# Attention scores: three 64-row products per head, the two heads in turn, in place of two 128-row products per head

## The chip, the core and the metric

The kernel runs on one core of a Trainium2 chip. TensorE multiplies: a load puts up to 128 rows by 128 columns of the first operand into the array, then the second operand streams through it, up to 512 columns, and the result goes to a bank of PSUM. VectorE, ScalarE and GpSimd do the rest of the arithmetic, and queues on SyncE, GpSimd and ScalarE issue DMAs. The metric is device time of one launch in microseconds (us), the median of several runs.

## What is computed

A trunk of two layers on 512 tokens of width 1024. Layer 0 mixes with an mLSTM (4 heads of 192) beside memory attention, layer 1 with band attention (12 heads of 64, on keys and values shared through one projection) beside memory attention. Memory attention has 4 heads of 64 and 256 memory tokens. Each mixer ends in an output projection, and a gated MLP with a short convolution follows. The part that concerns us, cut from the reference:

```python
# band attention, per chunk of queries (own chunk and 8 before)
s = jnp.einsum('bqhd,bkhd->bhqk', qc, kc).astype(jnp.float32) * scale + bias
s = jnp.where(valid, s, -jnp.inf)
p = jax.nn.softmax(s, axis=-1).astype(vc.dtype)
...
# memory attention
s = jnp.einsum('bshd,bmhd->bhsm', q, mk).astype(jnp.float32) * (MEM_HEAD_DIM ** -0.5)
p = jax.nn.softmax(s, axis=-1).astype(mv.dtype)
```

With at most 512 tokens and a band of 9 chunks of 64, every query sees all earlier keys, so band attention works here as causal attention by blocks.

## The kernel before

Activations stay transposed: a tile has 128 features on the partitions and the 512 tokens along the free axis. A float32 value is carried as two parts of a shorter format (type `fp32r`), a high part and the remainder, and a product of two float32 operands becomes three products: high by high, high by low, low by high (`mm3`, L192). Weights come in by DMA, ScalarE casts the high part and VectorE subtracts for the low one (`split`, L139, its two operations L140 and L141), and TensorE runs through hundreds of such triples (L194, L195, L196).

A head of 64 features fills only half of the 128 rows. Two heads share one tile of queries and one of keys: head 0 on partitions 0 to 63, head 1 on 64 to 127 (`HEADS`). The kernel before fills the array with the parts. `head_keys` (L587) builds for each head one tile that holds the keys' high part on the head's own half and the low part on the other. `head_queries` (L577) builds for each head two tiles: the high part of the queries on both halves, and the low part on the head's own half with zeros (a GpSimd memset, L580) on the other. `head_scores` (L594) then needs two products over 128 rows: the first gives high by high plus high by low, the second low by high. One block of scores, that is one token tile of 128 queries for both heads, is four products at L600, called by `scores` (L633): first both of head 0, then both of head 1, each head into its own bank of PSUM (pool tag `sc`, three banks).

Who calls it:

- `memory_attention` (L638), four times, with 256 keys. It works in two rounds of two token tiles (`softmax`, L646); both tiles of a head go to one bank, and the softmax on VectorE and ScalarE (L654 to L660) starts when both are there.
- `band_attention` (L1389), six times, once for each pair of heads, with token tile T reading the first (T + 1) x 128 keys: 128, 256, 384 and 512 columns. VectorE adds the bias and takes the maximum (L1406), ScalarE takes the exponential (L1410).
- The mLSTM heads call `head_scores` directly for the tile that two heads share, with keys and queries swapped. The change leaves these calls, `head_keys` and `head_queries` in place for them.

Queries come from `queries` (L625): those of layer 0 straight from PSUM, those of layer 1 first multiplied by a row of the norm. Keys come from `project_pair` (L1365, band) and `load_memory_kv` (L602, memory).

The order of work: each attention is a generator whose `yield`s mark places where filler may go. `weave(job, filler, each)` runs the job and after each yield lets `each` times the yielded number (1 for a bare `yield`) of filler steps be issued; the filler is projection products, mostly triples for other tiles. The order in which this issues the operations is not the last word: outside the stages marked `manual_schedule` the compiler's planner reorders each engine's instructions by its own reckoning of when operands and buffers are ready, so that projection products may come between the four products of a block.

Of the kernel before, what the change touches and what calls it, by code (L numbers as in the profile page):

```python
# [10 lines left out]
F32R = mybir.dt.float32r  # L11
I32 = mybir.dt.int32
AF = mybir.ActivationFunctionType
ALU = mybir.AluOpType
AX = mybir.AxisListType

P = 128
D = 1024
S = 512
# [7 lines left out]
HD = 64  # L27
# [22 lines left out]
def f(ap):  # L50
    return ap.bitcast(F32)
# [3 lines left out]
def trunk(  # L55
# [18 lines left out]
    nc = tc.nc  # L74
    V, A, G = nc.vector, nc.scalar, nc.gpsimd
# [14 lines left out]
    def sb(tag, shape, dtype=F32):  # L90
        count[0] += 1
        return pool.tile(shape, dtype, tag=tag, name=f"{tag}{count[0]}", bufs=bufs[tag])

    def ps(tag):
        count[0] += 1
        return psum.tile([P, S], F32, tag=tag, name=f"p{tag}{count[0]}", bufs=pbufs[tag])
# [6 lines left out]
    def small(n=4, dtype=F32):  # L103
        smalls[0] += 1
        i = smalls[0] % 26
        return sb("s0" if i < 6 else "s1" if i < 12 else "s2", [P, 16], dtype)[:, :n]
# [28 lines left out]
    HEADS = (slice(0, HD), slice(HD, P))  # L135
# [3 lines left out]
    def split(hi, lo, src, on_act=True, pinned=False):  # L139
        high = A.copy(hi, src) if on_act else V.tensor_copy(hi, src)  # L140
        low = V.tensor_tensor(out=lo, in0=src, in1=f(hi), op=ALU.subtract)  # L141
        if pinned:
            pin(high)
            pin(low)
# [53 lines left out]
    def project(w, c0, act, tag="mm"):  # L198


        n = len(act)
        wh, wl = weights(rows(w, c0, P), n, P)
        o = ps(tag)
        for k in range(n):
            mm3(o, wh[:, k, :], wl[:, k, :], act[k][0], act[k][1], k == 0, k == n - 1)
            yield
        return o
# [250 lines left out]
    def value_weights(hf, u):  # L458
        n = AW // 2
        ex = rows(a_w_in, 4 * AW, 2 * AH, 2 * u, 2 * u + 2) if hf else None  # L460
        return load(rows(a_w_in, 2 * AW + hf * n, n, 2 * u, 2 * u + 2), 2, n, ex)

    with tc.manual_schedule(engines={mybir.EngineType.PE, mybir.EngineType.Activation, mybir.EngineType.DVE}):
# [56 lines left out]
        for q in range(KT // 2):  # L520
            k = 2 * q
# [39 lines left out]
        raw = value_weights(1, 0)  # L561
# [15 lines left out]
    def head_queries(t, scale=1.0):  # L577
        qs, ls = ([sb("u", [P, S], F32R) for _ in range(2)] for _ in range(2))
        for h, r in enumerate(HEADS):
            G.memset(f(ls[h])[HEADS[1 - h], :], 0.0)  # L580
            A.activation(qs[h][r, :], t[r, :], AF.Copy, scale=scale)
            V.scalar_tensor_tensor(ls[h][r, :], t[r, :], scale, f(qs[h])[r, :], op0=ALU.mult, op1=ALU.subtract)
        for h, r in enumerate(HEADS):
            A.copy(qs[h][HEADS[1 - h], :], f(qs[h])[r, :])
        return qs, ls

    def head_keys(t):  # L587
        ks = [sb("u", [P, S], F32R) for _ in range(2)]
        for h, r in enumerate(HEADS):
            A.copy(ks[h][r, :], t[r, :])  # L590
            V.tensor_tensor(out=ks[h][HEADS[1 - h], :], in0=t[r, :], in1=f(ks[h])[r, :], op=ALU.subtract)
        return ks

    def head_scores(o, h, q, tsl, k, c, first, keys_first=False):  # L594

        for i, part in enumerate(q):
            a, b = part[h][:, tsl], k[h][:, c]
            if keys_first:
                a, b = b, a
            nc.tensor.matmul(o, a, b, start=first and i == 0, stop=i == 1)  # L600

    def load_memory_kv(l):  # L602
        raw = sb("wr", [P, D])
        nc.sync.dma_start(raw, spill[l])
        k = head_keys(raw[:, :S])
        vs = []
        for m in range(2):
            v = sb("u", [P, S], F32R).rearrange("p (h c) -> p h c", h=4)
            src = raw[:, S + m * MEM : S + (m + 1) * MEM].rearrange("p (h c) -> p h c", h=4)
            split(v[:, :, :HD], v[:, :, HD:], src)  # L610
            vs.append(v)
        return k, vs


    def values(outs):

        s, t = sb("t", [P, S]), sb("t", [P, S])
        for o, r in zip(outs, HEADS):
            A.copy(t[r, :], o[HD:, :])
            V.tensor_tensor(out=s[r, :], in0=o[:HD, :], in1=t[r, :], op=ALU.add)  # L620
        hi, lo = sb("u", [P, S], F32R), sb("u", [P, S], F32R)
        split(hi, lo, s)
        return hi, lo

    def queries(o, row):  # L625

        if row is None:
            return head_queries(o, HD**-0.5)
        q = sb("t", [P, S])
        V.scalar_tensor_tensor(q, o, HD**-0.5, row, op0=ALU.mult, op1=ALU.mult)  # L630
        return head_queries(q)

    def scores(outs, q, tsl, k, c):  # L633

        for h in range(2):
            head_scores(outs[h], h, q, tsl, k, c, True)

    def memory_attention(q, kv, hp, mixes):  # L638

        k, vs = kv  # L640
        pts = [sb("pt", [P, 5 * S], F32R) for _ in range(2)]
        pth = [p[:, : 2 * S].rearrange("p (a t) -> p a t", a=2) for p in pts]
        ptl = [p[:, 2 * S : 4 * S].rearrange("p (a t) -> p a t", a=2) for p in pts]
        es = {}

        def softmax(T2):  # L646
            ss = [ps("sc").rearrange("p (t m) -> p t m", t=2) for _ in range(2)]
            for i in range(2):
                T = 2 * T2 + i
                scores([s[:, i, :] for s in ss], q, slice(T * P, (T + 1) * P), k, slice(hp * MEM, (hp + 1) * MEM))  # L650
                yield
            for h in range(2):
                mx, sm = small(2), small(2)
                V.tensor_reduce(mx, ss[h], axis=AX.X, op=ALU.max, negate=True)  # L654
                e = sb("t", [P, S]).rearrange("p (t m) -> p t m", t=2)
                for i in range(2):
                    A.activation(e[:, i, :], ss[h][:, i, :], AF.Exp, bias=mx[:, i : i + 1], accum_out=sm[:, i : i + 1])
                V.reciprocal(sm, sm)
                for i in range(2):
                    V.tensor_scalar(e[:, i, :], e[:, i, :], sm[:, i : i + 1], None, op0=ALU.mult)  # L660
                es[T2, h] = e
                yield

        def transposed(T2):
            for h in range(2):
                tp = ps("tr").rearrange("p (a t c) -> p a t c", a=2, t=2)
                for i in range(2):
                    for a in range(2):
                        nc.tensor.transpose(tp[:, a, i, :], es[T2, h][:, i, a * P : (a + 1) * P], ident)  # L669
                tsl = slice(2 * T2 * P, 2 * (T2 + 1) * P)  # L670
                split(pth[h][:, :, tsl], ptl[h][:, :, tsl], tp.rearrange("p a t c -> p a (t c)"))
                yield

        yield from softmax(0)
        yield from softmax(1)
        yield from transposed(0)
        yield from transposed(1)
        outs = []
        for h in range(2):
            o2 = ps("tr")  # L680
            outs.append(o2)
            for i, (a, p) in enumerate(((0, pth), (0, ptl), (1, pth), (1, ptl))):
                nc.tensor.matmul(o2, vs[a][:, 2 * hp + h, :], p[h][:, a, :], start=i == 0, stop=i == 3)
            yield
        mixes[6 + hp] = values(outs)
        yield
# [396 lines left out]
    e, u, c, r = (cpool.tile([P, TT, AH], F32, name=f"gate{i}") for i in range(4))  # L1083
# [255 lines left out]
    for j in range(KT):  # L1339
        wh, wl = weights(rows(ffn_w_down[0], j * P, P, FT - LAST, FT), LAST, P)  # L1340
        o = ps("mm")
# [23 lines left out]
    def project_pair(j):  # L1365
        def times_row(o):
            t = sb("t", [P, S])
            V.tensor_tensor(out=t, in0=o, in1=norm.row, op=ALU.mult)
            return t

        ov = yield from project(w_kv, AW + j * P, kvact)
        t = times_row(ov) if norm.row is not None else None
        o = yield from project(w_kv, j * P, kvact)
        if t is None:
            t = times_row(ov)
        k = head_keys(times_row(o))
        tp = ps("mm")
        for T in range(TT):
            nc.tensor.transpose(tp[:, T * P : (T + 1) * P], t[:, T * P : (T + 1) * P], ident)
        v = []  # L1380
        for i in range(2):

            w = sb("u" if j == 5 else ("fh", "fl")[i], [P, S], F32R).rearrange("p (h c) -> p h c", h=4)
            split(w[:, :, :HD], w[:, :, HD:], tp[:, i * MEM : (i + 1) * MEM].rearrange("p (h c) -> p h c", h=4))
            v += [w[:, :2, :], w[:, 2:, :]]
        q = queries((yield from project(b_w_in, j * P, act)), norm.row)
        qkv[j] = q, k, v
# [132 lines left out]
    for hf in range(2):  # L1520
# [6 lines left out]
        for Ts, pieces in groups:  # L1527
            for c in pieces:
                if c.start:
                    os_[Ts[0]] = ps("mm")  # L1530
                for u in range(n):
# [4 lines left out]
                    for T in Ts:  # L1536
                        for i in range(2):
                            k = 2 * u + i
# [58 lines left out]
```

## Time and profile before

| | us |
|---|---|
| Median of 3 runs | 1179.24 (1179.14 to 1179.31) |
| The profiled execution | 1178.82 |
| Its span | 1177.1 |

The profile is of one execution. Instructions carry a start, a duration and the line of the source that issued them; a matmul's duration includes its way through the array, so that durations of neighbours overlap, and the cost of one is better read from start to start. PE is the matmuls, PEld the loads of the first operand. "128*128 128x256" of a matmul reads: 128 rows by 128 columns loaded, 256 columns streamed. The groups that concern the change, all of L600 or of the preparation of its operands:

| Line | Engine, operation | Count | Mean, ns |
|---|---|---|---|
| L600 | TensorE, 256 columns | 96 | 287 |
| L600 | TensorE, 512 columns | 32 | 401 |
| L600 | TensorE, 384 columns | 32 | 339 |
| L600 | TensorE, 128 columns | 32 | 271 |
| L581 | ScalarE, high part of a query (from SBUF) | 20 | 628 |
| L590 | ScalarE, high part of a key (from SBUF) | 16 | 619 |

### The profile page before, as it was taken

To read this page: it belongs to the slowest core of one execution; us is meant where nothing else is said; L and a number is where in the kernel's file an instruction comes from. 1 tells how busy PE (TensorE), PEld (TensorE's weight loads), DVE (VectorE), ACT (ScalarE), POOL (GpSimd) and SP (SyncE) were. 2 spreads that over 40 slices of the span, in tenths; PEclk is the share of its full clock that TensorE was granted. 3 is DMA by queue.
4 is the path that set the end of the run, shared out by engine and by line. 5 is a ranking of instruction groups with operands and counts; after the bars stand their busy time and mean duration, and the time that the engine had idled before them with its cause. 6 is when DMAs were issued, how large, how long until landed. Compare 5 with 4: busy or idle time off the path is not lost.

```text
span 1177.1 us, 18647 instructions
## 1 busy us (share of the span) xinstructions
PE 1167.3 (99%) x7005; PEld 1032.8 (88%) x7005; DVE 940.8 (80%) x1680; ACT 728.9 (62%) x1297; POOL 129.2 (11%) x222
## 2 busy tenths in 40 slices
PE   9999999999999999999999999999999999999997
PEld 9988888888889999999888888778889999999986
DVE  6777788887979878877688888897897887777755
ACT  6548677655656655666666677676565665666545
POOL 1111101010021121111020000101001011110100
PEclk9999999999999999999999999999999999999999
DMA  8645325243366766665563313325426466666551
GB/s 285 222 112 141 85 55 152 76 144 116 90 161 158 181 167 163 163 145 125 155 205 114 90 54 96 105 90 179 141 90 153 108 137 143 142 144 144 126 161 72
DMA packets 199420, 158.64 MB, mean 135 GB/s; under 512 B 8376, under 2 KB 178334, under 8 KB 199330
## 3 DMA queue, kind: packets, MB, share of 16 engines
q1 hardware_dynamic: 183170, 119.87, 34.6%
q0 software_dynamic: 15584, 36.67, 15.7%
q8 instruction: 55, 0.90, 0.3%
q10 hardware_dynamic: 576, 0.92, 0.2%
q14 instruction: 35, 0.29, 0.1%
HBM read 128.89 MB, written 32.46 MB: 137 GB/s over the span
## 4 chain that ended last, share of the span: by engine, by line
PE 95%; ACT 2%; DVE 2%; issue 0%; POOL 0%; POOLq 0%; DVEq 0%; ACTq 0%
PE pmm L194 18%; PE pmm L195 18%; PE pmm L196 18%; PE ptr L195 6%; PE ptr L194 6%; PE ptr L196 6%; PE psc L196 5%; PE psc L195 5%; PE psc L194 5%; PE psc L600 2%; PE ptr L1421 1%; PE ptr L1442 1%; PE ptr L1443 1%; PE ptr L669 0%; PE pmm L491 0%; PE pmm L470 0%
## 5 line engine op out<-in xcount | busy, mean ns | idle before, releaser
L194 PE MATMUL pmm<-u,wh 128*128 128x512 f32 (+1 forms) x968 | 333.2, 345 | 0.3 <-ACT u L140 0.3
L196 PE MATMUL pmm<-u,wl 128*128 128x512 f32 (+1 forms) x968 | 330.6, 342 | 0.0
L195 PE MATMUL pmm<-u,wh 128*128 128x512 f32 (+1 forms) x968 | 330.4, 341 | 0.0
L141 DVE TENSOR_TENSOR wl<-wr,wh 128x1024 fp32r<-128x1024 f32 (+3 forms) x172 | 199.7, 1162 | 83.0 <-ACT wh L140 81.5
L140 ACT CAST wh<-wr 128x1024 fp32r<-128x1024 f32 (+3 forms) x172 | 171.8, 1001 | 91.8 <-PE pmm L195 40.8
L196 PEld LDWEIGHTS pmm<-u,wl 128*128 128x128 f32 x968 | 181.8, 188 | 20.7
L194 PEld LDWEIGHTS pmm<-u,wh 128*128 128x128 f32 x968 | 181.8, 188 | 18.7 <-ACT u L140 1.2
L195 PEld LDWEIGHTS pmm<-u,wh 128*128 128x128 f32 x968 | 182.0, 188 | 18.1 <-DVE u L141 0.5
L194 PE MATMUL ptr<-u,wh 128*128 128x512 f32 x272 | 106.4, 391 | 0.0
L195 PE MATMUL ptr<-u,wh 128*128 128x512 f32 x272 | 106.2, 390 | 0.0
L196 PE MATMUL ptr<-u,wl 128*128 128x512 f32 x272 | 105.8, 389 | 0.0
L834 POOL DMA_DIRECT2D xspill<-t x64 | 55.5, 868 | 428.8 <-ACT t L833 416.3
L890 ACT COPY t<-pmm 128x256 f32<-128x256 f32 x102 | 38.2, 374 | 76.7 <-PE pmm L196 76.5
L141 DVE TENSOR_TENSOR u<-t,u 128x512 fp32r<-128x512 f32 (+1 forms) x94 | 54.0, 595 | 35.3 <-ACT u L140 35.3
L194 PE MATMUL pmm<-u,fh 128*128 128x256 f32 x272 | 75.4, 277 | 0.0
L194 PE MATMUL psc<-u,wh 128*128 128x256 f32 (+1 forms) x232 | 75.3, 324 | 0.0
L195 PE MATMUL pmm<-u,fh 128*128 128x256 f32 x272 | 75.2, 276 | 0.0
L196 PE MATMUL pmm<-u,fl 128*128 128x256 f32 x272 | 75.1, 276 | 0.0
L196 PE MATMUL psc<-u,wl 128*128 128x256 f32 (+1 forms) x232 | 75.1, 324 | 0.0
L195 PE MATMUL psc<-u,wh 128*128 128x256 f32 (+1 forms) x232 | 74.9, 323 | 0.0
L141 DVE TENSOR_TENSOR fl<-pt,fh 128x512 fp32r<-128x512 f32 x102 | 70.2, 689 | 5.1 <-ACT fh L140 1.4
L140 ACT CAST fh<-pt 128x512 fp32r<-128x512 f32 x102 | 62.8, 616 | 8.3 <-DVE pt L944 4.9
(352 smaller groups left out, 2494.6 us busy)
## 6 DMA issues: line engine op xcount, KB each, us to landing
wr<-in_ffn_w_up_dram SPq DMA_DIRECT2D x54, 512.0 KB, 6.3
wr<-in_ffn_w_down_dram SPq DMA_DIRECT2D x38, 512.0 KB, 5.4
pt<-in_ffn_w_up_dram SPq DMA_DIRECT2D x34, 512.0 KB, 8.2
xspill<-t POOLq DMA_DIRECT2D x64, 256.0 KB, 4.3
wr<-in_a_w_in_dram SPq DMA_DIRECT2D x20, 512.0 KB, 3.9
wr<-in_w_kv_dram SPq DMA_DIRECT2D x12, 512.0 KB, 4.1
xspill<-fh POOLq DMA_DIRECT2D x16, 256.0 KB, 2.6
xspill<-fl POOLq DMA_DIRECT2D x16, 256.0 KB, 2.9
```

The source lines that it names most:

```text
L140: high = A.copy(hi, src) if on_act else V.tensor_copy(hi, src)
L141: low = V.tensor_tensor(out=lo, in0=src, in1=f(hi), op=ALU.subtract)
L194: nc.tensor.matmul(o, lh, rh, start=first, stop=False, skip_group_check=more)
L195: nc.tensor.matmul(o, lh, rl, start=False, stop=False, skip_group_check=more)
L196: nc.tensor.matmul(o, ll, rh, start=False, stop=last, skip_group_check=more)
L600: nc.tensor.matmul(o, a, b, start=first and i == 0, stop=i == 1)
L834: G.dma_start(xspill[j], t, accum_op=ALU.add)
L890: A.copy(o, r[:, :H])
L1421: nc.tensor.transpose(tp[:, b * P : (b + 1) * P], es[T, h][:, b * P : (b + 1) * P], ident)
L1442: nc.tensor.matmul(o2[:, s * P :], w, hi_at(pts[h], s, s, TT - s), start=s == 0, stop=False)
L1443: nc.tensor.matmul(o2[:, s * P :], w, lo_at(pts[h], s, s, TT - s), start=False, stop=s == TT - 1)
```

## The change

The parts are no longer stacked. A new helper, `pair_parts`, splits a whole tile of two heads into a high and a low tile with one ScalarE and one VectorE operation each over all 128 partitions; it replaces `head_queries` and `head_keys` for band and memory attention. `scores` now issues, for a block, six products over 64 rows: high by high, high by low and low by high, each for head 0 (rows 0 to 63) and then for head 1 (rows 64 to 127). In memory attention the yield between the two token tiles of a round now gives 0 filler steps, and the one after the second tile gives twice as many, so that both tiles' scores are issued in one run.

```diff
+    def pair_parts(t, scale=1.0):
+
+        hi, lo = (sb("u", [P, S], F32R) for _ in range(2))
+        A.activation(hi, t, AF.Copy, scale=scale)
+        V.scalar_tensor_tensor(lo, t, scale, f(hi), op0=ALU.mult, op1=ALU.subtract)
+        return hi, lo
+
...
     def load_memory_kv(l):
         raw = sb("wr", [P, D])
         nc.sync.dma_start(raw, spill[l])
-        k = head_keys(raw[:, :S])
+        k = pair_parts(raw[:, :S])
...
     def queries(o, row):
 
         if row is None:
-            return head_queries(o, HD**-0.5)
+            return pair_parts(o, HD**-0.5)
         q = sb("t", [P, S])
         V.scalar_tensor_tensor(q, o, HD**-0.5, row, op0=ALU.mult, op1=ALU.mult)
-        return head_queries(q)
+        return pair_parts(q)
 
     def scores(outs, q, tsl, k, c):
 
-        for h in range(2):
-            head_scores(outs[h], h, q, tsl, k, c, True)
+        for i, (a, b) in enumerate(((0, 0), (0, 1), (1, 0))):
+            for o, r in zip(outs, HEADS):
+                nc.tensor.matmul(o, q[a][r, tsl], k[b][r, c], start=i == 0, stop=i == 2)
...
                 scores([s[:, i, :] for s in ss], q, slice(T * P, (T + 1) * P), k, slice(hp * MEM, (hp + 1) * MEM))
-                yield
+                yield 2 * i
...
-        k = head_keys(times_row(o))
+        k = pair_parts(times_row(o))
```

## The prediction

> **What bounds the kernel now.** I read the page first: the busy shares, the granted clock and the chain that ended last.
>
> ```profile
> span 1177.1 us, 18647 instructions
> ...
> PE 1167.3 (99%) x7005; PEld 1032.8 (88%) x7005; DVE 940.8 (80%) x1680; ACT 728.9 (62%) x1297; POOL 129.2 (11%) x222
> ...
> PE 95%; ACT 2%; DVE 2%; issue 0%; POOL 0%; POOLq 0%; DVEq 0%; ACTq 0%
> ```
>
> TensorE carries 95% of the chain. So a change here is worth what it does to the array's queue, and work taken from the other engines counts only where the array waits for them. How often it does, the stage windows show (columns: window and length, then busy time and instructions of each engine, clock, DMA share, GB/s). The scores that the change touches lie in these two:
>
> ```profile
> 150.00:250.00 100.00, 99.69 (x506) 83.26 (x504) 80.16 (x176) 67.82 (x123) 6.09 (x14) 1.00 0.34 97
> 630.00:795.00 165.00, 163.88 (x851) 135.04 (x851) 143.67 (x366) 116.16 (x274) 11.83 (x22) 1.00 0.29 88
> ```
>
> TensorE is idle for 0.31 us of the first and 1.12 us of the second: 1.43 us is all that faster helpers can give back in visible idle time.
>
> Next, the line of the scores by source: minimum, median and maximum duration, then the shapes.
>
> ```profile
> L600 PEld LDWEIGHTS psc<-u,u x192: 186/188/192, 103.9 to 794.3; 128*128 128x128 f32 x192
> L600 PE MATMUL psc<-u,u x192: 220/283/496, 104.2 to 794.6; 128*128 128x256 f32 x96, 128*128 128x512 f32 x32, 128*128 128x384 f32 x32, 128*128 128x128 f32 x32
> ```
>
> Of the 192 products, 32 belong to the mLSTM heads and stay (four heads, four blocks, two products). 96 are band attention's: 6 pairs, 4 token tiles, 4 products of 128, 256, 384 and 512 columns. 64 are memory attention's: 4 calls, 4 token tiles, 4 products of 256 columns. A matmul's duration includes its passage through the array, so I price by slots, from one start to the next, in the timeline (start, duration, engine, line).
>
> ```profile
> 656.94 0.64 PE L600 MATMUL psc<-u,u 128*128 128x128 f32 x4
> 657.42 0.45 PE L194 MATMUL pmm<-u,wh 128*128 128x512 f32 x1
> 657.71 0.39 PE L195 MATMUL pmm<-u,wh 128*128 128x512 f32 x1
> 657.93 0.39 PE L196 MATMUL pmm<-u,wl 128*128 128x512 f32 x1
> 658.16 0.64 PE L600 MATMUL psc<-u,u 128*128 128x256 f32 x4
> 658.63 0.40 PE L194 MATMUL pmm<-u,wh 128*128 128x512 f32 x1
> ...
> 661.63 0.88 PE L600 MATMUL psc<-u,u 128*128 128x384 f32 x4
> 662.35 0.39 PE L194 MATMUL pmm<-u,wh 128*128 128x512 f32 x1
> ...
> 665.57 1.09 PE L600 MATMUL psc<-u,u 128*128 128x512 f32 x4
> 666.49 0.39 PE L194 MATMUL pmm<-u,wh 128*128 128x512 f32 x1
> ...
> 769.51 1.11 PE L600 MATMUL psc<-u,u 128*128 128x256 f32 x8
> 770.47 0.40 PE L194 MATMUL pmm<-u,wh 128*128 128x512 f32 x1
> ```
>
> Four products hold the array for 0.54 us at 128 columns (0.48 us, and the next projection product then holds it 0.29 instead of 0.23 us), 0.47 at 256, 0.72 at 384 and 0.92 at 512; eight of memory attention hold it 0.96 us. One slot is thus about 0.12, 0.18 and 0.23 us for 256, 384 and 512 columns. The touched scores cost 6 x 2.65 + 8 x 0.96 = 23.6 us now.
>
> **The products themselves.** Each block goes from four products over all 128 rows to six over 64 rows, alternating between the two halves of the array. The trace has no 64-row product, so I bound a pair (one of each head): at best its two streams and its two weight loads run at once and it takes one slot, at worst two. For the weight loads I need this stretch, which also holds the only products of the kernel that use fewer than 64 rows, eight 4-row transposes:
>
> ```profile
> 85.67 0.39 PE L194 MATMUL pmm<-u,wh 128*128 128x512 f32 x1
> 85.68 0.19 PEld L195 LDWEIGHTS pmm<-u,wh 128*128 128x128 f32 x1
> ...
> 86.13 0.39 PE L196 MATMUL pmm<-u,wl 128*128 128x512 f32 x1
> 86.44 0.13 PEld L1167 LDWEIGHTS ptr<-ident,t 4*128 4x128 f32 x1 [0.35 <-issue]
> 86.45 0.22 PE L1167 MATMUL ptr<-ident,t 4*128 4x4 f32 x1
> ...
> 86.90 0.20 PE L1168 MATMUL ptr<-ident,t 4*128 4x4 f32 x1
> 87.03 0.19 PEld L194 LDWEIGHTS pmm<-u,wh 128*128 128x128 f32 x1
> 87.03 0.50 PE L194 MATMUL pmm<-u,wh 128*128 128x512 f32 x1
> 87.14 0.19 PEld L195 LDWEIGHTS pmm<-u,wh 128*128 128x128 f32 x1
> 87.37 0.39 PE L195 MATMUL pmm<-u,wh 128*128 128x512 f32 x1
> ```
>
> Two loads follow each other by 0.11 us (87.03 to 87.14), so a pair takes at least 0.11 us. I take the best case for the pair: the two halves read different partitions and write different PSUM banks. Three pairs then take 0.33, 0.36, 0.54 and 0.69 us, 1.92 in place of 2.65, which saves 0.73 x 6 = 4.4 us in band attention. In memory attention six pairs for two token tiles take 0.72 in place of 0.96 us, 0.24 x 8 = 1.9 us. **Gain: 6.3 us.**
>
> **Changing the array's shape.** The load for L195 starts at 85.68, as soon as the product before its own has started: in plain work loads hide behind streaming. The 4-row load does not. It starts at 86.44, when the stream of the product before it (from 86.13, one slot of 0.23) has been over for 0.08 us, and the profile puts the gap down to no wait. On the way back L194's load starts at 87.03, 0.13 us after the last 4-row product, and L195 follows at 87.37. From 86.13 to 87.37 are 1.24 us; two 512-column slots (0.46) and eight 4-row ones ((86.90 - 86.45) / 7 = 0.064 each, 0.51) leave **0.27 us** for going out of the full shape and back.
>
> The Trainium skill's page "TensorEngine Tiling (Array Packing)", section "Tiling Modes", states that a change of tiling mode drains the array. By that rule each excursion into 64-row products pays as this 4-row one did; the trace agrees for 4 rows, and shows nothing for 64.
>
> For 64 rows I add the first load, 0.11 us, which at 256 columns and more would have been hidden: 0.38 us. At 128 columns loads set the pace anyway and 0.27 stays. The bounds are 0 (if halves and whole mix freely) and 0.38; I take the upper one, since the nearest row shows an empty array on both sides. Least number of excursions: 24 in band attention and 8 in memory attention, where the second yield rule puts two token tiles into one run (16 otherwise). 6 x 0.27 + 26 x 0.38 = **11.5 us**.
>
> **Runs that come apart.** The order on TensorE is the planner's, and where head 1's PSUM bank is not free in its reckoning it sets projection products between:
>
> ```profile
> 682.97 0.40 PE L600 MATMUL psc<-u,u 128*128 128x256 f32 x2
> 683.21 0.39 PE L194 MATMUL pmm<-u,wh 128*128 128x512 f32 x1
> ...
> 684.13 0.40 PE L600 MATMUL psc<-u,u 128*128 128x256 f32 x2
> ...
> 756.63 0.51 PE L600 MATMUL psc<-u,u 128*128 128x256 f32 x2 [0.33 <-DVE s L1406]
> ...
> 785.48 0.40 PE L600 MATMUL psc<-u,u 128*128 128x256 f32 x2
> ...
> 787.34 0.40 PE L600 MATMUL psc<-u,u 128*128 128x256 f32 x2
> ```
>
> These are the first break and parts of the last two in band attention. Breaks stand in 6 of the 24 band runs (four at 256 columns, one at 384, one at 512) and in 5 of the 16 token tiles of memory attention. With heads in turn, a break leaves head 0's three products alone on half of the array and head 1's likewise: another excursion, and no pair. Band: 6 x 0.38 + 4 x 0.36 + 0.54 + 0.69 = 5.0 us; memory, with both token tiles of head 0 ahead: 5 x (0.38 + 0.72) = 5.5 us. If all breaks stay that is 10.5 us, if none, nothing. The helpers get lighter, so banks come free a little earlier: I take half, **5.2 us**. Where the planner leaves head 1's first product second in the queue and its bank is late, everything behind it waits, projection products included; the like of it today is one wait of 0.33 us on L1406.
>
> **Lighter helpers.** Eight key preparations and ten query preparations change.
>
> ```profile
> L584 ACT CAST u<-u 64x512 fp32r<-64x512 f32 x24 | 14.9, 620 | 0.6
> L582 DVE SCALAR_TENSOR_TENSOR u<-t,u 64x512 fp32r<-64x512 f32 x20 | 13.7, 683 | 0.4
> L590 ACT CAST u<-t 64x512 fp32r<-64x512 f32 x16 | 9.9, 619 | 0.2
> L591 DVE TENSOR_TENSOR u<-t,u 64x512 fp32r<-64x512 f32 x16 | 11.0, 686 | 1.0 <-ACT u L590 0.6
> L580 POOL MEMSET u<- 64x512 f32 x24 | 12.6, 524 | 137.9 <-PE psc L600 69.9 <-PE pmm L195 40.1 <-ACT t L1410 23.0
> ```
>
> A query goes from four ScalarE operations to one, from two VectorE ones to one, and loses both memsets; a key loses one of each. ScalarE sheds (30 + 8) x 0.62 = 23.6 us, VectorE 18 x 0.69 = 12.4 us, GpSimd 20 x 0.52 = 10.5 us, and each query holds two buffers less. None of it is on the path: of the array's 1.43 idle us I give back half, **0.7 us** (bounds 0 and 1.4). On GpSimd's queue the bias loads no longer stand behind memsets that wait for buffers; they come earlier, and no TensorE wait is on them.
>
> **Sum.** -6.3 + 11.5 + 5.2 - 0.7 = +9.7 us. The profiled execution took 1178.82 us (span 1177.1 and 1.7 around it), 0.42 below the median of 1179.24: the profiled time becomes 1188.5, the median **1188.9 us**. With no break and all idle time back it is +3.8 us (1183.0), with every break and none back +15.7 (1194.9): 1183 to 1195 is this case's own range.
>
> **Rivals.** *Faster, since a change of shape is cheap for halves.* The 4-row run changed shape for tiny transposes; a half may need no empty array. Without breaks the change breaks even at (6.3 + 0.7) / 32 = 0.22 us per excursion, and below that it gains. At 0 to 0.1 us and no breaks it comes to -7.7 to -3.8 us: 1171.5 to 1175.4. For it speaks that no 64-row row exists in the trace; against it, 87.03.
>
> The same page, "Theoretical Speedup", allows up to 2x for a contraction of 64 or less. By that alone this rival would be the forecast; no run here shows it.
>
> *Break-even.* 0.2 to 0.25 us per excursion and few breaks: within 2.4 us of before, about 0.2%, which is what a measurement of this kernel can tell from no change.
>
> *The weight loads take turns.* If one loader serves both halves, a pair takes 2 x 0.11 = 0.22 us (0.23 at 512 columns). Three pairs: 0.66, 0.66, 0.66, 0.69, together 2.67 against 2.65; memory attention: 1.32 against 0.96, 2.9 us. The gain of 6.3 turns into a loss of 3.0; breaks then cost mainly their excursions (2.1 for half): 3.0 + 11.5 + 2.1 - 0.7 = +15.9, 1195.1 us. For it speaks that loads are busy 88% of the span.
>
> The skill's page "TensorE: Matmul & The Clock Gate", section "LDWEIGHTS (loading the stationary operand)", gives columns / 1.2 ns whatever the rows, 107 ns here. By it a half-height load is no cheaper than the 0.11 us of this trace, which agrees for 128 rows.
>
> *The pairs don't overlap at all* (the change doesn't do what it says). Six slots: 0.66, 0.72, 1.08, 1.38, together 3.84 against 2.65, 7.1 us; memory attention 1.44 against 0.96, 3.8 us. 10.9 + 11.5 + 2.1 - 0.7 = +23.8, 1203.0 us.
>
> **How the numbers follow.** Forecast 0.46, loads in turn 0.14, no overlap 0.09, faster 0.22, break-even 0.09. Slower is 0.46 + 0.14 + 0.09 = 0.69. The range for 8 in 10 goes from 1174 (half of the faster case left out) to 1202 (most of the no-overlap case left out).
>
> **What would show it.** Right: in the timeline, pairs of 64-row products whose starts lie under 0.02 us apart, pair after pair by one slot; behind each run the first projection load starting only after the run's last product, with some 0.2 us lost there and some 0.2 before the run; about 240 products on the scores' line in 32 to 43 runs. Wrong: projection loads that start before the run ends (cheap shape change), pairs spaced by 0.22 us at 256 columns (loads in turn) or singles by 0.12 (no overlap). The forecast fails if excursions cost under 0.25 us, or if the order breaks in far more places than today.

## The result, and the profile after

| | before | after |
|---|---|---|
| Median, us | 1179.28 (1179.14 to 1179.93) | 1188.64 (1188.37 to 1189.05) |
| The profiled execution, us | 1178.82 | 1188.73 |
| Its span, us | 1177.1 | 1187.0 |

The change costs 9.4 us: a ratio of 1.0082, 95% interval 1.0069 to 1.0095. The forecast was 1188.9.

The page of the changed kernel, the lines that answer to those shown of the kernel before:

```profile
span 1187.0 us, 18715 instructions
...
PE 1178.3 (99%) x7085; PEld 1029.6 (87%) x7085; DVE 928.9 (78%) x1662; ACT 703.6 (59%) x1259; POOL 120.2 (10%) x202
...
PE 93%; issue 5%; ACT 1%; DVE 1%; POOL 0%; POOLq 0%; ACTq 0%; DVEq 0%
```

ScalarE lost 25 us of work, VectorE 12 and GpSimd 9, much as forecast, and the span grew. New in the chain is "issue", 5%, some 57 us: time in which the last chain waited for nothing that the profile shows. It doesn't measure the change. Most of it is one stretch of the chain, which starts at 143.45:

```profile
143.45 46.25 issue
```

TensorE was busy for all of these 46.25 us. What the change does to the array shows in the scores' new line by source:

```profile
L644 PEld LDWEIGHTS psc<-u,u x240: 182/184/189, 156.7 to 803.8; 64*128 64x128 f32 x120
L644 PE MATMUL psc<-u,u x240: 272/322/498, 156.7 to 804.1; 64*128 64x256 f32 x66, 64*128 64x128 f32 x18, 64*128 64x384 f32 x18, 64*128 64x512 f32 x18
...
  issue: 11.9, 36
```

(The matmul row's shapes are of pairs of load and product; there are 132, 36, 36 and 36 products.) 36 times the array or its loader sat idle ahead of a 64-row product, 11.9 us in all, with no other engine to blame. There are 41 runs of such products. Now the timeline at the same pair of heads that the prediction read:

```profile
660.91 0.39 PE L196 MATMUL pmm<-u,wl 128*128 128x512 f32 x1
661.23 0.55 PE L644 MATMUL psc<-u,u 64*128 64x128 f32 x6
661.71 0.50 PE L194 MATMUL pmm<-u,wh 128*128 128x512 f32 x1
662.05 0.39 PE L195 MATMUL pmm<-u,wh 128*128 128x512 f32 x1
662.27 0.40 PE L196 MATMUL pmm<-u,wl 128*128 128x512 f32 x1
662.60 0.62 PE L644 MATMUL psc<-u,u 64*128 64x256 f32 x6
663.16 0.50 PE L194 MATMUL pmm<-u,wh 128*128 128x512 f32 x1
...
666.03 0.40 PE L196 MATMUL pmm<-u,wl 128*128 128x512 f32 x1
666.36 0.80 PE L644 MATMUL psc<-u,u 64*128 64x384 f32 x6
667.08 0.50 PE L194 MATMUL pmm<-u,wh 128*128 128x512 f32 x1
667.42 0.39 PE L195 MATMUL pmm<-u,wh 128*128 128x512 f32 x1
```

Before each run the 512-column product holds the array 0.32 or 0.33 us in place of 0.23, and behind it the first one holds it 0.34. The records of single products in this trace start in twos, 96 of them, most 0.003 or 0.004 us apart and none over 0.015, and twos of 256 columns end 0.12 us after each other. So the pairs work, and going there and back eats more than they give. The loads show the same borders:

```profile
666.36 0.47 PEld L644 LDWEIGHTS psc<-u,u 64*128 64x128 f32 x6 [0.37 <-issue]
667.08 0.19 PEld L194 LDWEIGHTS pmm<-u,wh 128*128 128x128 f32 x1 [0.25 <-issue]
667.19 0.19 PEld L195 LDWEIGHTS pmm<-u,wh 128*128 128x128 f32 x1
```

The first load of the new shape starts only with its product, on the way out and on the way back; the next one (667.19) is ahead of its product again.

The stage windows, to be read against those of before (the second is 10 us longer, so that it holds about the same work):

```profile
150.00:250.00 100.00, 99.87 (x510) 81.31 (x510) 77.42 (x172) 63.28 (x116) 5.66 (x12) 1.00 0.34 97
630.00:805.00 175.00, 174.66 (x933) 134.38 (x932) 135.91 (x356) 97.08 (x247) 5.46 (x10) 1.00 0.29 88
```

TensorE's visible idle time in the two stages fell from 1.43 to 0.47 us.

**An account of the array.** For every run below I took each product's step, from the end of the product before it to its own end, out of all 7,000 or so records. A whole product (128 rows) with another before it has a standard step by its columns: I used 0.228, 0.174, 0.114 and 0.110 us for 512, 384, 256 and 128. What a step takes beyond it I put into one of two bins: "out and back" for the first product of a 64-row run and the first whole one behind it, "waits" for the rest. "Scores" are the touched scores' own steps: standard ones where they are whole products, those measured inside the runs otherwise. "Waits" is a remainder: steps that are long for another reason are in it too, as those behind 128-column products, and its level hangs on the third digit of the standard steps (0.227 and 0.113 us for 512 and 256, the medians to the nanosecond, put some 6 us more into it in every row). Only its differences between rows can be read; they come out the same within 0.2 us either way.

| Kernel | median, us | 64-row runs | scores | out and back | waits |
|---|---|---|---|---|---|
| before | 1179.28 | 0 | 22.3 | 0 | 13.4 |
| after | 1188.64 | 41 | 20.4 | 15.8 | 9.4 |
| helpers alone | 1176.86 | 0 | 22.3 | 0 | 11.6 |
| whole-array products | 1190.16 | 0 | 33.5 | 0 | 13.1 |
| one 64-row product per block | 1193.35 | 40 | 22.3 and 4.4 | 13.4 | 9.9 |
| one head after the other | 1190.37 | 39 | 19.6 | 15.2 | 12.5 |
| both heads on one half | 1201.83 | 41 | 34.7 | 15.6 | 8.4 |
| bare yield | 1189.71 | 46 | 19.4 | 18.0 | 9.1 |
| held together | 1186.62 | 40 | 17.3 | 15.3 | 10.9 |
| tiles 0 and 1 joined | 1186.43 | 35 | 20.5 | 13.4 | 9.5 |
| held together and joined | 1184.63 | 34 | 17.7 | 12.9 | 11.2 |
| all that PSUM allows joined | 1182.96 | 24 | 17.7 | 9.7 | 12.4 |

The first two rows add up to the difference of the spans: -1.9 + 15.8 - 4.0 = +9.9 us.

### The profile page after: what moved, and what is told of

It reads as the page before. It is cut to its first block, busy times and chain, and to the rows that moved or that the text cites. A ratio compares the mean times of both kernels' runs of the same rounds, so it can differ in the third digit from the quotient of the medians.

```text
span 1187.0 us, 18715 instructions
## 1 busy us (share of the span) xinstructions
PE 1178.3 (99%) x7085; PEld 1029.6 (87%) x7085; DVE 928.9 (78%) x1662; ACT 703.6 (59%) x1259; POOL 120.2 (10%) x202
## 4 chain that ended last, share of the span: by engine, by line
PE 93%; issue 5%; ACT 1%; DVE 1%; POOL 0%; POOLq 0%; ACTq 0%; DVEq 0%
PE pmm L194 18%; PE pmm L195 17%; PE pmm L196 17%; PE ptr L195 6%; PE ptr L194 6%; PE ptr L196 6%; PE psc L196 5%; PE psc L195 5%; PE psc L194 5%; PE psc L644 2%; PE ptr L1429 1%; PE ptr L1451 1%; PE ptr L1450 1%; PE ptr L691 1%; PE ptr L677 0%
## 5 line engine op out<-in xcount | busy, mean ns | idle before, releaser
L194 PE MATMUL pmm<-u,wh 128*128 128x512 f32 (+1 forms) x968 | 336.3, 348 | 0.2 <-ACT u L140 0.2
L194 PEld LDWEIGHTS pmm<-u,wh 128*128 128x128 f32 x968 | 181.7, 188 | 24.1 <-issue 2.7
L194 PE MATMUL ptr<-u,wh 128*128 128x512 f32 x272 | 106.4, 391 | 0.0
L194 PE MATMUL pmm<-u,fh 128*128 128x256 f32 x272 | 75.4, 277 | 0.0
L194 PE MATMUL psc<-u,wh 128*128 128x256 f32 (+1 forms) x232 | 75.2, 324 | 0.0
```

The lines of the kernel that those rows point to most:

```text
L194: nc.tensor.matmul(o, lh, rh, start=first, stop=False, skip_group_check=more)
```

## The experiments

The kernel before ran again beside each group: 1178.86, 1178.90 and 1178.92 us. Diffs are against the changed kernel, and where they say so against the kernel before.

**Both heads on one half.** Is the overlap real, and what is it worth?

```diff
         for i, (a, b) in enumerate(((0, 0), (0, 1), (1, 0))):
-            for o, r in zip(outs, HEADS):
+            for o in outs:
+                r = HEADS[0]
                 nc.tensor.matmul(o, q[a][r, tsl], k[b][r, c], start=i == 0, stop=i == 2)
```

> The changed kernel with both heads' products reading head 0's partitions, so that all six of a block lie on the same half of the array (head 1's scores are then those of head 0; the time doesn't depend on that). Same number of products, same 41 runs in the same written order. This is the test of the overlap that the run with one head after the other turned out not to be, since the two halves started together there too. My theory (halves work at the same time): 96 pairs become single slots, 43 x 0.117 + 17 x 0.11 + 18 x 0.174 + 18 x 0.228 = 14.1 us, of which a few tenths to 2 us may be soaked up by waits that it covers: 1200.5 to 1202.7 us. Rival (the overlap is worth nothing, loads or PSUM set the pace): 1188.6.

1201.83 us, 13.2 above the changed kernel. The same 41 runs stand in the same places and pay the same 15.6 us for out and back; only the scores' steps went from 20.4 to 34.7 us. A run of six at 256 columns in its timeline:

```profile
665.78 0.40 PE L196 MATMUL pmm<-u,wl 128*128 128x512 f32 x1
666.11 0.98 PE L645 MATMUL psc<-u,u 64*128 64x256 f32 x6
667.01 0.50 PE L194 MATMUL pmm<-u,wh 128*128 128x512 f32 x1
```

0.90 us from the run's start to the next product, where the changed kernel's run at 662.60 takes 0.56. The overlap of the two halves is shown: nothing else differs, and the whole loss lies inside the runs.

**One head after the other.** This was meant to take the overlap away, and didn't.

```diff
-        for i, (a, b) in enumerate(((0, 0), (0, 1), (1, 0))):
-            for o, r in zip(outs, HEADS):
+        for o, r in zip(outs, HEADS):
+            for i, (a, b) in enumerate(((0, 0), (0, 1), (1, 0))):
```

> The changed kernel with the two loops of the scores swapped: all three 64-row products of head 0, then all three of head 1. Same products, same shape changes (the written order has 39 runs of 64-row products, the changed kernel 41), no two neighbours on different halves except where one head ends and the next begins. My theory (overlap of neighbours on different halves saves a slot for each pair, a shape change costs 0.40 us per run): the 96 pairs that the changed kernel's trace shows start together turn into single slots, 43 x 0.117 + 17 x 0.11 + 18 x 0.174 + 18 x 0.228 = 14.1 us, less one pair per block that may still meet where the heads change, and less 2 x 0.4 us for two runs fewer: about 1198 to 1202 us. Rival (the overlap saves nothing, the loss is elsewhere): within 2 us of the changed kernel's 1188.6.

1190.37 us, close to the rival's number but not for the rival's reason. The run of 384 columns takes as long as in the changed kernel (666.36 to 667.08):

```profile
667.05 0.80 PE L644 MATMUL psc<-u,u 64*128 64x384 f32 x6
667.78 0.19 PEld L194 LDWEIGHTS pmm<-u,wh 128*128 128x128 f32 x1 [0.25 <-issue]
```

Its six single records start at 667.050, 667.060, 667.332, 667.342, 667.510 and 667.520. The program has head 0's three ahead of head 1's, and the planner kept them so in this run; the load of the second record is the one that carries the wait for head 1's bank, and the last two are the ones that signal an end. So head 1's first product started 0.010 us after head 0's first, ahead of head 0's second and third: inside a run the halves run as two queues, and 0.010 us in place of the changed kernel's 0.003 or 0.004 is in keeping with three places in the program in place of one. The account agrees: 97 pairs, 19.6 us of scores. What the run lost against the changed kernel is 3.1 us in waits; its list of TensorE's waits is headed by this:

```profile
PE ptr L1429 <- DVE pt L141: 1.7, 5, 0.5
```

The planner's order differs there. That this wait is the whole of it isn't shown.

**One 64-row product in the kernel before.** The shape change alone, with the old helpers and the old products; the diff is against the kernel before.

```diff
+        r, n = HEADS[0], slice(c.start, c.start + P)
+        nc.tensor.matmul(outs[0][:, :P], q[0][0][r, tsl], k[0][r, n], start=True, stop=True)
         for h in range(2):
             head_scores(outs[h], h, q, tsl, k, c, True)
```

> The kernel before, with one 64-row product of 128 columns ahead of each block of scores (40 in all, its output is overwritten by the block). The shape change alone. My theory: each costs its slot of 0.11 us and 0.34 us for going out of the full shape and back (0.14 before it, 0.20 behind it, as at the changed kernel's runs of 128 columns), 40 x 0.45 = 18 us: 1197 us. Rival (a half mixes freely with whole products): 40 x 0.11 = 4.4 us, 1183.7 us.

1193.35 us: 14.5 over the kernel before where I expected 18 and the rival 4.4. The 40 excursions cost 13.4 us and their slots 4.4, which is the 18; but the waits fell from 13.4 to 9.9 us, though no helper was touched. About half of this fall lies at the blocks themselves, where a wait ahead of the 64-row product now counts as way out; 1.8 us lie at other products. Time added to the array thus seems to cover waits that were there before; that it does so wait by wait isn't shown.

**Whole-array products.** Six products per block with no shape change and no overlap.

```diff
+            G.memset(f(hs[h])[HEADS[1 - h], :], 0.0)
+            G.memset(f(ls[h])[HEADS[1 - h], :], 0.0)
...
-            for o, r in zip(outs, HEADS):
-                nc.tensor.matmul(o, q[a][r, tsl], k[b][r, c], start=i == 0, stop=i == 2)
+            for h, o in enumerate(outs):
+                nc.tensor.matmul(o, q[a][h][:, tsl], k[b][:, c], start=i == 0, stop=i == 2)
```

> The changed kernel with its six products per block over all 128 rows: each head has a high and a low query tile whose other half is zero (four memsets on GpSimd per query), keys as in the changed kernel. No shape changes and no overlap. My theory: 240 single slots, 132 x 0.117 + 36 x 0.11 + 36 x 0.174 + 36 x 0.228 = 33.9 us against the 25.4 us that the 160 products of the kernel before hold the array, so +8.5, 1187 to 1188 us, and projection products behind a run hold their usual 0.23 us. Rival (six products in alternation are dear by themselves, whatever the shape): the price of the runs stays, 16 us more, above 1200 us.

1190.16 us, 2 to 3 more than expected. The scores' 33.5 us are as reckoned; the waits stayed at 13.1, so added time does not always cover waits. My sum had set them off: it counted the old products at the 25.4 us for which they hold the array, waits among them, where their standard steps make 22.3, and the new ones without waits. Both mechanisms thus land within 2 us of each other: paying for the second half of the array, or paying for the way there. The border is gone, as this timeline shows:

```profile
660.09 0.39 PE L196 MATMUL pmm<-u,wl 128*128 128x512 f32 x1
660.32 0.78 PE L654 MATMUL psc<-u,u 128*128 128x128 f32 x6
660.94 0.44 PE L194 MATMUL pmm<-u,wh 128*128 128x512 f32 x1
661.22 0.40 PE L195 MATMUL pmm<-u,wh 128*128 128x512 f32 x1
```

**The helpers alone.**

```diff
-        for i, (a, b) in enumerate(((0, 0), (0, 1), (1, 0))):
-            for o, r in zip(outs, HEADS):
-                nc.tensor.matmul(o, q[a][r, tsl], k[b][r, c], start=i == 0, stop=i == 2)
+        for o in outs:
+            for i in range(2):
+                nc.tensor.matmul(o, q[i][:, tsl], k[0][:, c], start=i == 0, stop=i == 1)
...
-                yield 2 * i
+                yield
```

> Only the lighter preparation of queries and keys, with the products as before the change: four per block over 128 rows, a bare yield after each token tile. The products mix the two heads' features, which the time doesn't depend on. My theory (the helpers are off the path): -0.5 to -1.4 us, about 1178.4. Rival (the lighter helpers free the array of stalls worth several us, and the change lost more than 9.4 us elsewhere): under 1176.

1176.86 us: 2.0 below the kernel before, ratio 0.9983 (0.9974 to 0.9992). This kernel mixes the two heads' features, so its time serves the argument alone. More than my -0.5 to -1.4, less than the rival's 3. TensorE's visible idle time in the two stages is 0.02 and 0.63 us here, 0.8 less than before; the account finds 1.8 us.

**The number of runs and the pairs.** Four kernels vary them. First, the changed kernel with the bare yield:

> The changed kernel with the bare yield between the two token tiles of memory attention. The written order then has 46 runs of 64-row products in place of 41. My theory (0.40 us per run): +2 us, 1190.6 us. Rival (the time does not go with the number of runs): 1188.6.

1189.71 us, 1.1 more, half of what I expected: 46 runs cost 2.2 us more for out and back, and 1.0 comes back in the scores, since a few more products met their partner (100 pairs for 96). Four executions of each kernel, which spread over 0.7 and 1.0 us, can just tell such a difference.

Second, each block held together, so that no planner's break separates the heads:

```diff
+        if not more:
+            c0 = slice(c.start, c.start + 4)
+            nc.tensor.matmul(outs[1][:4, :4], q[0][:, tsl.start : tsl.start + 4], k[0][:, c0], start=True, stop=True)
         for i, (a, b) in enumerate(((0, 0), (0, 1), (1, 0))):
             for o, r in zip(outs, HEADS):
-                nc.tensor.matmul(o, q[a][r, tsl], k[b][r, c], start=i == 0, stop=i == 2)
+                pin(nc.tensor.matmul(o, q[a][r, tsl], k[b][r, c], start=i == 0, stop=i == 2))
```

> The changed kernel with each block's six products held together: a 128-row product of 4 by 4 columns to head 1's bank comes first (about 0.03 us), and the six are pinned in order behind it, so that they start only when both banks are free. 40 runs in the written order in place of 41, but head 0's and head 1's products stand next to each other also in memory attention. My theory: of the 23 pairs of 256 columns that came apart some 20 are regained, 20 x 0.117 = 2.3 us, one run fewer is 0.4, the small products cost 32 x 0.03 = 1.0: about 1186.9 us. Rival (the lone halves cost nothing, since another engine sets the pace there): 1188.6 to 1189.6.

1186.62 us. The scores' steps fell by 3.1 us, close to what pairing everything leaves (below, 16.7): the lone halves did cost time.

Third, the first two token tiles of band attention in one run, in one bank per head; fourth, that and the one before together (the last argument of `scores` only there):

```diff
+            banks = [ps("sc") for _ in range(2)]
...
+            for T in Ts:
+                n = (T + 1) * P
+                ss = [o[:, at : at + n] for o in banks]
+                scores(ss, q, slice(T * P, n), k, slice(0, n), at > 0)
...
-        yield from softmax(0)
-        yield from softmax(1)
+        yield from softmax(0, 1)
```

> The changed kernel with the first two token tiles of band attention joined alone, nothing held together. 35 runs in place of 41. My theory: -6 x 0.37 = -2.2 us, 1186.4 us. Rival as before: 1188.6 or more.

> The same, and in band attention the first two token tiles (128 and 256 columns) share a head's bank and go in one run of twelve products. 34 runs. My theory: 1186.9 less 6 x 0.37 us, about 1184.5 us. Rival (joining delays the softmax of the first tile, and the array waits for it): no gain over the run before it, 1187 or more.

1186.43 and 1184.63 us: both within 0.2 us of what I expected from the price per run.

**All that PSUM allows.** If fewer runs are better, how far does that go? Token tiles 2 and 3 in one run and memory attention's four in one, with a fourth bank taken from the transposes:

```diff
-            ss = [ps("sc").rearrange("p (t m) -> p t m", t=2) for _ in range(2)]
+            tags = ["sc", "sc", "sc", "tr"]
+            banks = [[ps(tags.pop(0)).rearrange("p (t m) -> p t m", t=2) for _ in range(2)] for _ in range(2)]
...
+        yield from softmax(0, 1)
+        yield from softmax(2, 3)
```

> The most runs joined that PSUM allows: in band attention token tiles 0 and 1 share banks as before and tiles 2 and 3 go in one run with a fourth bank borrowed from the transposes; in memory attention all four token tiles go in one run. Held together as in the run of 34. 24 runs in the written order. My theory: 10 runs fewer than the 34 at 0.39 us, -3.9 us, about 1180.7 us, still not below the kernel before. Rival (scores in bursts keep the banks longer, and the array waits for the softmax): 1183 or more.

1182.96 us, between my 1180.7 and the rival's 1183 and nearer to the rival's. Out and back fell by 3.2 us, and 1.2 came back as waits, of which TensorE's list has this one that the changed kernel's has not:

```profile
PE ptr L1443 <- DVE s L1426: 1.0, 5, 0.3
```

It is still 4.0 us slower than the kernel before (1.0034, 1.0020 to 1.0047). Its timeline shows a pair by name, since head 1's bank is one of the transposes' there:

```profile
662.82 0.39 PE L647 MATMUL psc<-u,u 64*128 64x512 f32 x1
662.82 0.39 PE L647 MATMUL ptr<-u,u 64*128 64x512 f32 x1
663.05 0.39 PE L647 MATMUL psc<-u,u 64*128 64x512 f32 x1
663.05 0.39 PE L647 MATMUL ptr<-u,u 64*128 64x512 f32 x1
```

Two products of 512 columns start in the same hundredth, and the next two 0.23 us later.

**Two tries on the kernel before.** Can the helpers' 2.0 us be had without the products? And is the yield rule worth something by itself? Both diffs are against the kernel before.

```diff
-            A.copy(qs[h][HEADS[1 - h], :], f(qs[h])[r, :])
+            G.tensor_copy(qs[h][HEADS[1 - h], :], f(qs[h])[r, :])
```

> The kernel before, with one thing taken from the finding that lighter helpers alone gave 2.0 us: the copy of the queries' high part to the other half (24 of 0.62 us on ScalarE) moves to GpSimd, which is busy 11% of the span. My theory: a part of the 2.0 us, -0.3 to -1.0: 1178.2 us. Rival (GpSimd is slower at it, the queries come later and VectorE is held up): 1179.5 or more.

1197.10 us, 18.2 slower. GpSimd's queue, not its time, is the reason that the waits name:

```profile
L584 POOL CAST u<-u x24: 608/930/1133, 94.6 to 786.1; 64x512 fp32r<-64x512 f32 x24
```

```profile
POOL u L584 <- ACT u L581: 174.8, 12, 32.6
...
DVE t L1406 <- DMA bias<-rep: 16.1, 8, 3.9
```

The copies wait in GpSimd's order for ScalarE, band attention's bias loads are issued by the same queue behind them, and VectorE then waits 16.1 us for those loads, a wait that the kernel before has not. TensorE waits in turn for L1406. In the account the waits rise from 13.4 to 32.8 us.

```diff
                 scores([s[:, i, :] for s in ss], q, slice(T * P, (T + 1) * P), k, slice(hp * MEM, (hp + 1) * MEM))
-                yield
+                yield 2 * i
```

> The kernel before with the changed yields of memory attention alone: both token tiles' scores in one run, products over 128 rows. My theory (whole products don't care what stands beside them): within 0.5 us of the kernel before. Rival (the grouping itself moves softmax and filler): 1 us or more either way.

1178.75 us against 1178.92, ratio 0.9998 (0.9989 to 1.0007): whole products don't care. Of the kernels that do the whole computation, none came out measurably faster than the kernel before.

## Why the prediction was right, term by term

**The pairs: right.** Forecast -6.3 us. Standard steps for 120 perfect pairs are 66 x 0.114 + 18 x (0.110 + 0.174 + 0.228) = 16.7 us, against 22.3 for the 160 products of before: -5.6. The run with both heads on one half shows that this is overlap. The rival with loads that take turns is out: pairs of 128 columns end 0.11 us apart, one load's time for two loads.

**The price of a shape change: right, and the row of eight 4-row transposes gave it.** Forecast 0.38 us at 256 columns and more, 0.27 at 128. Measured, in the changed kernel: 0.20 before the run and 0.20 behind it, 0.40; at 128 columns 0.14 and 0.20, 0.34. The small one was low by 0.07. Over all runs it is 15.8 / 41 = 0.39 us, and 0.38 to 0.40 in the four kernels with 46, 35, 34 and 24 runs.

The drain that the Trainium skill's "TensorEngine Tiling (Array Packing)", section "Tiling Modes", states for a change of tiling mode thus holds for 64 rows too: 0.40 us there and back by this trace.

**The breaks: right in kind, low in size and wrong in place.** I took half of those in the old order, 5.2 us, split between band and memory attention. In the changed kernel band attention has one (a block of 128 columns, cut into 1, 2 and 3), and memory attention has 15 runs in place of 8, with 23 pairs come apart. Runs and lone halves together cost 15.8 + (20.4 - 16.7) = 19.5 us, where the forecast had 11.5 + 5.2 = 16.7.

**The relief: -4.0 us by the account, where I forecast -0.7 and at most -1.4.** Two steps failed. First, I read the ceiling off TensorE's idle time in the windows. A product's duration (0.39 us at 512 columns) is longer than its slot (0.23), so the busy time hides up to 0.16 us of every wait; the helpers alone took 2.0 us off the time, more than the 1.43 that I had called all. The view of the old scores by source had more than the windows show, 2.9 us of idle time ahead of its loads and products, the mLSTM's among them:

```profile
its engine sat idle before it (us, times) until:
  DVE s L1406: 1.0, 2
  ACT t L657: 0.6, 2
  ACT u L584: 0.5, 2
  DVE u L591: 0.5, 1
  issue: 0.3, 1
```

Second, I tied relief to the helpers. They alone give 1.8 us of it; one 64-row product per block gives 3.5 us without any. The two overlap, and how the 4.0 us divide between them stays open.

Where the 4.0 lay can be said. About 3.1 us of it were long steps at the touched scores themselves, in the old kernel, between the products of a block, ahead of it or right behind it; eight of 0.1 to 0.6 us make 2.1 of them. These products held the array for 22.3 + 3.1 = 25.4 us, where my sum started from 23.6. In the changed kernel a step at a run's border belongs to "out and back", and all of these but one lie between 0.14 and 0.21 us over the standard step, so the old waits are gone there, under a price that is paid in any case. At all other products the steps fell by 0.9 us in sum, close to the 0.7 of the forecast.

So the total was met with some luck. The scores and their borders went from 25.4 to 20.4 + 15.8 = 36.2 us, where I had 23.6 and 34.0: both ends were low by about 2 us, and the difference, +10.8 against +10.4, came out nearly right. Of the rivals, the cheap shape change failed at its own test, L194's load at the run's end (667.08, 0.25 us idle with nothing to wait for). No kernel here had few enough runs for break-even: at 24 runs the pairs give 4.6 us (22.3 - 17.7) and the way there and back costs 9.7.

## What to carry to other kernels

Price an array shape change as a bubble on both sides, here 0.40 us, and compare it with what one stay in the new shape saves, here 0.23 us for a block that fills two PSUM banks of 512 columns: by these two numbers overlap of small products pays only if a stay holds about two such blocks, four banks' worth, or more (an estimate; no kernel here came out ahead). Look for one instruction of the wanted shape anywhere in the old trace; eight tiny transposes gave this price. When the bound engine gets slower, waits that it had can vanish under the added time (3.5 us of 18 with one 64-row product per block, next to nothing with whole-array products), so take a sum of added terms as an upper bound, and read the engine's waits from step to step, not from busy time.

## What I had not expected of the hardware

The two halves of the array are not tied to program order within a run. In the kernel with one head after the other, with head 0's three products ahead of head 1's, head 1's first started 0.010 us after head 0's first and ahead of its second and third.

The Trainium skill's "TensorE: Matmul & The Clock Gate", section "The mechanism", has matmuls start and end in strict program order, with weight loads alone moved ahead. For products on different halves the records here differ from that (667.050 and 667.060, then 667.332). Products on the same half show nothing against it.
